# Attention scores from queries and keys split into a high and a low part: three fp32r products in place of one fp32 product

## The chip, the core and the metric

The kernel runs on one NeuronCore of one Trainium2 chip. The number that counts is the time of one execution in device microseconds (us), as the median of several runs. Engines are named as in the profile: PE is the matrix engine, PEld its weight loads, DVE the vector engine, ACT the scalar engine, POOL the GpSimd engine, and SP the engine that issues most of the DMAs. Each engine works through its own queue in order, and engines wait for each other by semaphores.

## What is computed

One layer of a hybrid backbone runs on 128 context tokens and 512 latent tokens (8 rows of 64) with 1024 channels. The modulated input goes through one wide projection. One branch is a gated long convolution. The other is attention with 16 heads of 64 channels: the context attends to itself, and each latent query attends to a window of the latent grid and to 128 cached context keys. The change concerns the scores of this attention:

```python
def context_attention(q, k, v):
    ...
    s = jnp.einsum("bqhd,bkhd->bhqk", q, k).astype(jnp.float32) * (HEAD_DIM ** -0.5)
    p = jax.nn.softmax(s, axis=-1).astype(v.dtype)
    ...

def neighbourhood_attention(q, k, v, ctx_k, ctx_v, rpb):
    ...
    s_win = jnp.einsum("brqhd,brkhd->bhrqk", qg, kg).astype(jnp.float32) * scale
    ...
    s_ctx = jnp.einsum("brqhd,bkhd->bhrqk", qg, ctx_k).astype(jnp.float32) * scale
    p = jax.nn.softmax(jnp.concatenate([s_win, s_ctx], axis=-1), axis=-1).astype(v.dtype)
```

The two branches are then gated, projected and merged (`m_h * p_h + m_a * p_a`), go through one more projection and a layer norm, and the keys and values of the context tokens are outputs too.

## The kernel before

**Projections in three products.** Every projection (`proj`, `accumulate`, line 165) multiplies a weight tile by the 640 tokens. Weights and input are each split into a high part, rounded to the type fp32r, and a low part, the rest (`split`, lines 97 and 98: ACT writes the high part, DVE subtracts it). The product is high by high, high by low and low by high, each an fp32r matmul of 320 columns, over eight blocks of 128 channels: 48 matmuls per projection. The result lies in one of two PSUM tiles `mm` (pool `ps_mm`, two buffers). So the projection after next starts only when ACT, or ACT and DVE, have emptied the tile of this one.

**Scores in one fp32 product.** Heads are worked on in pairs j = 0 to 7; the two heads of a pair lie in partitions 0 to 63 and 64 to 127 of the tiles `q{j}` and `k{j}`. `queries(j)` (line 666) copies the projection from PSUM into `q{j}` in four ACT operations with the factor -0.125; `keys(j)` (lines 674 to 678) copies it into `k{j}` in five, loads the cached keys by two DMAs straight into two places of `k{j}`, and sends the context's keys out from `k{j}` by a DMA. `score` (line 756) is one matmul per head with 64 rows and fp32 operands; the profile shows every fp32 matmul as two records. A pair has four blocks of 128 queries (`KWIN`: 320, 384, 384 and 320 keys) and the context's block of 128 keys. `tiled` issues the scores of two blocks; the softmax (`probs`: DVE, ACT, POOL) follows, and `turned` transposes its result on PE one step later.

**Stages.** The order of PE is written by hand only in the prologue and in the eight steps of attention, where `weave` mixes `attend(j)` with the projections of later pairs (`mains`). Elsewhere, and on the other engines, a list scheduler orders the instructions by the order of the program and by when a simulation finds them ready. Before the attention comes the hand-over: `hand_over()` runs the last tiles of the convolution branch (`quarter_tail(3)`), then `queries(0)`, `keys(0)`, `values(0)`, `gate_a(0)`, `queries(1)`, `keys(1)`, `values(1)`. It is woven with the last quarter of the long convolution (`long_conv(3)`, `long_conv_back(3)`) and with `attention_setup()`. The tail of `long_conv_back(3)` is two transposes `yp` (line 603), eight transposes `y` (line 613), and then DVE alone: lines 606, 615, and the gating at 451 and 455.

**Memory.** SBUF is given out in pools on two stacks, left and right. A tile of a new pool whose bytes belonged to closed pools waits, by the framework's rule, for the last use of those pools as a whole. On the left lie `const`, `wp` (raw, high and low weights), `yhp`, and `hwa`, the convolution's smaller pool, some 24.6 KB per partition by its tile sizes. On the right lie `hp` (the input) and below it `hyc` and `hw`, the convolution's large tiles, closed by `hy.close()` at the start of `attention_setup`. Once `hwa` is closed, its place is taken by `slots_l` (even pairs and j = 0) and `slots_r` (odd pairs), each with one tile q, k and v: 2560 + 3584 + 5120 = 11264 bytes per partition. Closing `hy` makes room for `yap` (attention's output) and `at` (its working tiles).

**After the attention.** `mix_h` puts the eight merge gates `mh0` to `mh7` into the q, k and v tiles of `slots_l` and into a pool `rest` of four tiles. The last loops split the outputs of both branches (`yhH`, `yhL`, `yaH`, `yaL`) and run the projections of the merge.

**Start.** `load_pack(1)` loads small constants in one DMA (428 columns) after the first slice of the input, ahead of `zemb`, which the filter network reads.

Of the kernel before, what the change touches and what calls it, by code (L numbers as in the profile page):

```python
# [9 lines left out]
F32 = mybir.dt.float32  # L10
# [6 lines left out]
LP = 128  # L17
# [27 lines left out]
def tile_hyena_natten_step(ctx: ExitStack, tc: tile.TileContext, a, o):  # L45
# [9 lines left out]
    def two(t):  # L55
        return t.rearrange("p (a b) -> p a b", a=2)
# [36 lines left out]
    def aux(name):  # L93
        return ps_ax.tile([P, 512], F32, tag="aux", name=name)
# [152 lines left out]
    def prologue():  # L247
# [27 lines left out]
        for k in range(NK):  # L275
# [382 lines left out]
    def slot(j, tag, name):  # L658
        pool = out["slots_l"] if j % 2 == 0 else out["slots_r"]
        return pool.tile([P, SLOT[tag]], F32, tag=tag, name=name)  # L660

    def queries(j):
        lo, hi, _ = yield from proj(T_Q + j)
        q = out[f"q{j}"] = slot(j, "q", f"q{j}")
        for dst, src in ((PS_, lo[:, PS_]), (blk(0, 2), lo[:, B01]), (blk(2, 5), hi[:, :HALF]), (blk(7, 1), lo[:, B7])):
            nc.scalar.activation(q[:, dst], src, AF.Copy, scale=-0.125)
        yield

    def keys(j):
        lo, hi, _ = yield from proj(T_K + j)  # L670
        k = out[f"k{j}"] = slot(j, "k", f"k{j}")
        for c in (192, 448):
            load_to(k[:, c : c + P], a["ck"][j])
        nc.scalar.activation(k[:, KP], lo[:, PS_], AF.Copy)
        nc.scalar.activation(k[:, 704:768], lo[:, B7], AF.Copy)
        nc.scalar.activation(k[:, :128], lo[:, B01], AF.Copy)
        nc.scalar.activation(k[:, 128:192], hi[:, :64], AF.Copy)
        nc.scalar.activation(two(k[:, 320:832])[:, :, :128], two(hi[:, 64:HALF]), AF.Copy)
        nc.sync.dma_start(o["new_kT"][j], k[:, KP])
        yield  # L680

    def values(m):
# [41 lines left out]
    def attention_setup():  # L724
        nonlocal at, mask
        hy.close()
        yap = out["yap"] = tail.enter_context(tc.tile_pool(name="yap", bufs=1, side="right"))
        ya.extend(row(yap, "ya", f"ya{j}") for j in range(NK))
        at = ac.enter_context(tc.tile_pool(name="at", bufs=1, side="right"))
        mask = at.tile([P, 640], F32, tag="mask", name="mask")  # L730
        load_to(mask[:], a["mask"])
        for i in range(4):
            tm = at.tile([P, 1024], F32, tag=f"tm{i}", name=f"tm{i}")
            for c in (192, 448, 704):
                nc.gpsimd.memset(tm[:, c : c + P], 0.0)
# [16 lines left out]
        nc.gpsimd.tensor_tensor(tm[:, 832:], mask[:, 448:], tb[:, :192], op=ALU.subtract)  # L752
        return tm

    def score(dst, q, k, h):
        nc.tensor.matmul(dst, q[rows(h)], k[rows(h)], start=True, stop=True, skip_group_check=True)  # L756

    def scores(j, b, s):
        lo, hi = KWIN[b]
        for h in range(2):  # L760
            score(s[h][:, : hi - lo], out[f"q{j}"][:, blk(2 * b, 2)], out[f"k{j}"][:, lo:hi], h)

    LIVE = (slice(64, 384), slice(0, 384), slice(0, 384), slice(0, 320))

# [39 lines left out]
    def block_scores(n, s):  # L804
        j, b = divmod(n, 4)
        if b == 0:
            cv = at.tile([P, P], F32, tag="cacheV", bufs=2, name=f"cv{j}")
            load_to(cv[:], a["cv"][:, j * P : j * P + P])
            head[j] = dict(cv=cv, tm=biases.pop(j))
            for h in range(2):  # L810
                score(s[h][:, 384:512], out[f"q{j}"][:, :LP], out[f"k{j}"][:, KP], h)
        scores(j, b, s)

    def block_probs(n, s):
# [85 lines left out]
        yield  # L900

    def mix_h():
        for n in range(NK):
            if n < 3:
                th = slot(0, "qkv"[n], f"mh{n}")
                if n == 2:
                    pair = th
                th = th[:, :NT]
            elif n == 3:
                th = pair[:, NT:]  # L910
            else:
                if n == 4:
                    out["rest"] = left.enter_context(tc.tile_pool(name="rest", bufs=1))
                th = out["rest"].tile([P, NT], F32, tag="mh", bufs=4, name=f"mh{n}")[:]
            ps = (yield from proj(T_MH + n))[2]
            nc.scalar.activation(two(th), ps[:, :, :HALF], AF.Tanh, scale=0.5)
            out[f"mh{n}"] = th
            yield
# [300 lines left out]
```

## Time and profile before

| what | value |
|---|---|
| median of 3 runs | 931.69 us (931.51 to 932.01) |
| the profiled execution, its own time | 931.77 us |
| span of its trace | 930.0 us |
| busy: PE, DVE, ACT, POOL | 914.6, 470.2, 378.5, 144.9 us |
| score matmuls (line 756) | 160 records, 80 matmuls |

The trace covers the span from the first to the last instruction; the execution's own time is 1.8 us longer. In the lists of groups, `x` is a count, and then come the busy time and the mean of one instruction. A matmul's duration in them is that of one alone, from its start until its result is there. As matmuls overlap, what one costs in a row of many is the row's time divided by the count. The chain of waits does this division: each piece begins where the one before it ended. In the timeline, `x4` merges four instructions that follow each other, and the bracket tells how long the engine was idle before, and for whom.

### The profile page before, as it was taken

Reading aid. Unit: us, or ns where it says so; the run is one execution under the profiler, and the core shown is the slowest. Engines: PE = TensorE matmul, PEld = TensorE weight load, DVE = VectorE, ACT = ScalarE, POOL = GpSimd, SP = SyncE. Lnnn points to the kernel's source line nnn. Section 1 sums busy time; section 2 is a strip of 40 time slices with the busy share of each in tenths; the row PEclk is TensorE's granted clock in tenths of the full one; section 3 lists DMA queues with packets and bytes.
Section 4 is the critical chain, followed back from the end, with each engine's and each line's share of the span. In section 5 each row is a group of like instructions: output and inputs, shape, how many; then the busy total and the mean of one; then the engine's idle time right before and its main releaser. Section 6 shows DMA issues by size and latency. Waiting matters only on the chain.

```text
span 930.0 us, 16507 instructions
## 1 busy us (share of the span) xinstructions
PE 914.6 (98%) x6785; PEld 873.0 (94%) x6785; DVE 470.2 (51%) x868; ACT 378.5 (41%) x769; POOL 144.9 (16%) x188
## 2 busy tenths in 40 slices
PE   9999999999999999999999999999999999999996
PEld 7899999999999999999989999999999999999885
DVE  4676775693796675334342432422171223335676
ACT  4485455555544324245454544444261112223300
POOL 0011010110010000464444443242000000000000
PEclk9999999999999999999999999999999999999999
DMA  9966564665465112342222211311123333223631
GB/s 345 349 159 133 128 148 97 134 135 123 100 144 121 57 49 76 100 116 62 59 89 72 66 65 48 92 50 55 60 69 99 132 115 117 84 69 114 204 113 68
DMA packets 37559, 102.63 MB, mean 110 GB/s; under 512 B 4428, under 2 KB 14028, under 8 KB 37485
## 3 DMA queue, kind: packets, MB, share of 16 engines
q1 hardware_dynamic: 33308, 86.88, 29.2%
q0 software_dynamic: 4032, 14.68, 9.7%
q8 instruction: 53, 0.87, 0.4%
q14 instruction: 22, 0.17, 0.1%
q10 hardware_dynamic: 144, 0.03, 0.0%
HBM read 97.90 MB, written 3.67 MB: 109 GB/s over the span
## 4 chain that ended last, share of the span: by engine, by line
PE 94%; DVE 3%; ACT 1%; DMA 1%; SPq 0%; issue 0%; POOLq 0%; POOL 0%; ACTq 0%
PE mm L165 65%; PE out L1043 6%; PE v L695 5%; PE s L756 3%; PE pt L793 2%; PE s L800 2%; PE ve L704 1%; DMA w<-fw 1%; DMA zemb<-zemb 1%; ACT hH L309 1%; PE yb L150 1%; PE yb L152 1%; PE yb L151 1%; PE gate L242 0%; PE fl L380 0%; PE fl L381 0%
## 5 line engine op out<-in xcount | busy, mean ns | idle before, releaser
L165 PE MATMUL mm<-hH,wh 128*128 128x320 f32 x1120 | 263.0, 313 | 2.3 <-ACT hH L309 1.4
L165 PE MATMUL mm<-hH,wl 128*128 128x320 f32 x1120 | 259.0, 310 | 1.1 <-DVE wl L98 1.1
L165 PE MATMUL mm<-hL,wh 128*128 128x320 f32 x1120 | 259.1, 310 | 0.0
L98 DVE TENSOR_TENSOR wl<-raw,wh 128x1024 fp32r<-128x1024 f32 x66 | 82.3, 1249 | 238.6 <-ACT wh L97 238.3
L165 PEld LDWEIGHTS mm<-hH,wh 128*128 128x128 f32 x1120 | 186.4, 188 | 8.7 <-issue 4.9
L165 PEld LDWEIGHTS mm<-hH,wl 128*128 128x128 f32 x1120 | 187.7, 188 | 2.2 <-DVE wl L98 1.8
L165 PEld LDWEIGHTS mm<-hL,wh 128*128 128x128 f32 x1120 | 188.0, 188 | 1.5 <-DVE hL L310 0.8
L97 ACT ACTIVATE wh<-raw 128x1024 fp32r<-128x1024 f32 x66 | 69.9, 1059 | 207.5 <-PE mm L165 101.3
L142 POOL DMA_DIRECT2D wl<-wall x28 | 24.4, 871 | 265.2 <-ACT wl L141 154.9
L143 ACT ACTIVATE wh<-raw 128x1024 fp32r<-128x1024 f32 x28 | 29.7, 1060 | 43.3 <-PE mm L165 43.2
L777 POOL TENSOR_SCALAR p<-p,sm 128x384 f32<-128x384 f32 x32 | 41.8, 1319 | 28.6 <-DVE sm L776 28.6
L1073 POOL TENSOR_TENSOR r<-r,bc 128x64 f32<-128x64 f32 x1 | 0.3, 322 | 249.8 <-ACT r L1072 249.8
L775 ACT ACTIVATE p<-p,sm 128x384 f32<-128x384 f32 x32 | 19.7, 616 | 40.8 <-DVE sm L772 40.6
L470 DVE SCALAR_TENSOR_TENSOR x<-zs,pack,x 128x641 f32<-128x641 f32 x32 | 28.2, 882 | 14.4 <-ACT x L468 14.4
L777 POOL TENSOR_SCALAR edge<-edge,sm 128x320 f32<-128x320 f32 x32 | 34.7, 1095 | 0.0
L795 ACT ACTIVATE pts<-pt 128x384 f32<-128x384 f32 x64 | 26.4, 500 | 15.7 <-PE pt L793 15.6
L141 ACT ACTIVATE wl<-raw 128x1024 fp32r<-128x1024 f32 x28 | 30.0, 1073 | 0.0
L165 PE MATMUL mm<-yhH,wh 128*128 128x320 f32 x128 | 29.9, 315 | 0.0
L165 PE MATMUL mm<-yhL,wh 128*128 128x320 f32 x128 | 29.1, 309 | 0.0
L165 PE MATMUL mm<-yhH,wl 128*128 128x320 f32 x128 | 29.1, 309 | 0.0
L165 PE MATMUL mm<-yaH,wl 128*128 128x320 f32 x128 | 29.1, 309 | 0.0
L165 PE MATMUL mm<-yaL,wh 128*128 128x320 f32 x128 | 29.1, 309 | 0.0
(326 smaller groups left out, 1643.0 us busy)
## 6 DMA issues: line engine op xcount, KB each, us to landing
raw<-wall SPq DMA_DIRECT2D x96, 512.0 KB, 3.7
wl<-wall POOLq DMA_DIRECT2D x28, 512.0 KB, 5.7
ada<-wada SPq DMA_DIRECT2D x16, 512.0 KB, 7.9
gate<-wada SPq DMA_DIRECT2D x8, 512.0 KB, 3.7
wo<-wall SPq DMA_DIRECT2D x8, 512.0 KB, 3.7
xt<-xT SPq DMA_DIRECT2D x8, 320.0 KB, 8.5
dec<-decay SPq DMA_DIRECT2D x20, 128.0 KB, 3.2
x<-xB SPq DMA_DIRECT2D x5, 512.0 KB, 3.7
```

What stands on the lines that cost most here:

```text
L97: hi = nc.scalar.activation(dst_h, src, AF.Copy)
L98: return hi, (eng or nc.vector).tensor_tensor(dst_l, src, f(dst_h), op=ALU.subtract)
L141: nc.scalar.activation(wl, raw[:], AF.Copy, scale=-1.0)
L142: nc.gpsimd.dma_start(wl, a["wall"][i], accum_op=ALU.add)
L143: nc.scalar.activation(wh, raw[:], AF.Copy)
L165: nc.tensor.matmul(ps[hf][:, :HALF], wt[k], x[:, hf * HALF : (hf + 1) * HALF], start=(i == 0 and k == 0), stop=(i == lead[2] and k == NK - ...
L470: nc.vector.scalar_tensor_tensor(d, zs[:, c : c + NG], convw[:, i, c : c + 1], d, op0=ALU.mult, op1=ALU.add)
L695: nc.tensor.matmul(ps[:, t // 2, t % 2 * 256 : t % 2 * 256 + 256], x[:, k, P * t : P * t + P], wk, start=first and t % 2 == 0, stop=last, ...
L756: nc.tensor.matmul(dst, q[rows(h)], k[rows(h)], start=True, stop=True, skip_group_check=True)
L777: nc.gpsimd.tensor_scalar_mul(pv, pv, sm[:, 2:3])
L795: nc.scalar.activation(ptS[:], pt[:, :384], AF.Copy)
L1043: ins = nc.tensor.matmul(dst, m[k][:, c0 : c0 + P], w[:, c : c + n], start=(first and k == 0), stop=(last and k == NK - 1), skip_group_che ...
```

## The change

The tiles `q{j}` and `k{j}` become fp32r tiles with the high part, and new tiles `ql{j}` and `kl{j}` take the low part. `queries` has three ACT operations and three DVE operations, `keys` five splits. The context's keys are copied once more by ACT to a tile `kp` for the output. The cached keys are loaded by one DMA into a `const` tile that shares its place with `pack1`, copied from there to both places by one ACT operation, and subtracted by two DVE operations. `score` issues six fp32r matmuls for a block, alternating between the heads.

The slots grow to five tiles, 17408 bytes per partition each. `slots_r` is opened after `gate_a(0)` instead of beside `slots_l`. `ya` has one buffer fewer, and the pool `rest` is gone: the gates `mh4` to `mh7` move into `ql`, `kl` of `slots_l` and `q`, `ql` of `slots_r`, and `yaL0` into `kl` of `slots_r`. The constants `convw`, `hyd` and `ident` become a third pack, loaded in the fourth step of the prologue.

```diff
 PACKS = (
     (("cc", 16), ("bss", 16), ("sel", 2)),
-    (("fs1", 2), ("fs2", 2), ("fw1", 64), ("fw2", 128), ("convw", 96), ("hyd", 8), ("ident", 128)),
+    (("fs1", 2), ("fs2", 2), ("fw1", 64), ("fw2", 128)),
+    (("convw", 96), ("hyd", 8), ("ident", 128)),
 )
...
-                out["convw"] = out["convw"].rearrange("p (i c) -> p i c", c=4)
...
+            if k == 3:
+                load_pack(2)
+                out["convw"] = out["convw"].rearrange("p (i c) -> p i c", c=4)
...
-    SLOT = dict(q=NT, k=896, v=5 * 256)
+    SLOT = dict(q=NT, ql=NT, k=896, kl=896, v=5 * 256)
...
+    def heads_of(t):
+        return two(t)[:, :, :P]
 
     def queries(j):
         lo, hi, _ = yield from proj(T_Q + j)
-        q = out[f"q{j}"] = slot(j, "q", f"q{j}")
-        for dst, src in ((PS_, lo[:, PS_]), (blk(0, 2), lo[:, B01]), (blk(2, 5), hi[:, :HALF]), (blk(7, 1), lo[:, B7])):
-            nc.scalar.activation(q[:, dst], src, AF.Copy, scale=-0.125)
+        q, ql = out[f"q{j}"], out[f"ql{j}"] = [slot(j, t, f"{t}{j}", F32R) for t in ("q", "ql")]
+        for cs, shape, src in (
+            (slice(0, 256), two, heads_of(lo[:, :384])), (slice(256, 576), whole, hi[:, :HALF]), (slice(576, NT), whole, lo[:, B7]),
+        ):
+            nc.scalar.activation(shape(q[:, cs]), src, AF.Copy, scale=-0.125)
+            nc.vector.scalar_tensor_tensor(shape(ql[:, cs]), src, -0.125, f(shape(q[:, cs])), op0=ALU.mult, op1=ALU.subtract)
         yield
 
     def keys(j):
+        raw = const.tile([P, 196], F32, tag="pack1", name=f"ck{j}")[:, :P]
+        load_to(raw, a["ck"][j])
         lo, hi, _ = yield from proj(T_K + j)
-        k = out[f"k{j}"] = slot(j, "k", f"k{j}")
-        for c in (192, 448):
-            load_to(k[:, c : c + P], a["ck"][j])
...
+        k, kl = out[f"k{j}"], out[f"kl{j}"] = [slot(j, t, f"{t}{j}", F32R) for t in ("k", "kl")]
+        for cs, shape, src in (
+            (slice(704, 768), whole, lo[:, B7]), (slice(0, 128), whole, lo[:, B01]), (slice(128, 192), whole, hi[:, :64]),
+            (slice(320, 832), heads_of, two(hi[:, 64:HALF])), (KP, whole, lo[:, PS_]),
+        ):
+            split(shape(k[:, cs]), shape(kl[:, cs]), src)
+        kp = const.tile([P, P], F32, tag="kp", name=f"kp{j}")
+        nc.scalar.activation(kp[:], lo[:, PS_], AF.Copy)
+        nc.sync.dma_start(o["new_kT"][j], kp[:])
+        nc.scalar.activation(heads_of(k[:, 192:704]), raw.unsqueeze(1).to_broadcast([P, 2, P]), AF.Copy)
+        for cs in (slice(192, 320), slice(448, 576)):
+            nc.vector.tensor_tensor(kl[:, cs], raw, f(k[:, cs]), op=ALU.subtract)
         yield
...
         out["slots_l"] = left.enter_context(tc.tile_pool(name="slots_l", bufs=1))
+        yield from chain(queries(0), keys(0), values(0), gate_a(0))
         out["slots_r"] = left.enter_context(tc.tile_pool(name="slots_r", bufs=1))
-        yield from chain(queries(0), keys(0), values(0), gate_a(0), queries(1), keys(1), values(1))
+        yield from chain(queries(1), keys(1), values(1))
...
-        ya.extend(row(yap, "ya", f"ya{j}") for j in range(NK))
+        ya.extend(row(yap, "ya", f"ya{j}", bufs=NK) for j in range(NK))
...
-    def score(dst, q, k, h):
-        nc.tensor.matmul(dst, q[rows(h)], k[rows(h)], start=True, stop=True, skip_group_check=True)
+    def score(dst, j, qs, ks):
+        q, ql, k, kl = (out[f"{t}{j}"] for t in ("q", "ql", "k", "kl"))
+        for i, (x, y) in enumerate(((q, k), (ql, k), (q, kl))):
+            for h in range(2):
+                nc.tensor.matmul(dst[h], x[rows(h), qs], y[rows(h), ks], start=i == 0, stop=i == 2, skip_group_check=True)
...
     def mix_h():
+        homes = ((0, "q"), (0, "k"), (0, "v"), (), (0, "ql"), (0, "kl"), (1, "q"), (1, "ql"))
         for n in range(NK):
...
+            th = slot(*homes[n], f"mh{n}") if homes[n] else th
+            th, pair = (pair[:, NT:], None) if n == 3 else (th[:, :NT], th)
...
-        yaL.append(row(out["yap"], "ya", f"yaL{n}", F32R))
-        split(yaH[n][:], yaL[n][:], ya[n][:])
+        yaL.append(row(out["yap"], "ya", f"yaL{n}", F32R, NK)[:] if n else slot(1, "kl", "yaL0", F32R)[:, :NT])
+        split(yaH[n][:], yaL[n], ya[n][:])
```

More of the change, by code (lines that the diff above doesn't have):

```diff
@@ L655, in tile_hyena_natten_step, with slot, whole @@
     PS_ = slice(PC, PC + LP)
-    SLOT = dict(q=NT, k=896, v=5 * 256)
-    def slot(j, tag, name):
+    SLOT = dict(q=NT, ql=NT, k=896, kl=896, v=5 * 256)
+    def slot(j, tag, name, dt=F32):
         pool = out["slots_l"] if j % 2 == 0 else out["slots_r"]
-        return pool.tile([P, SLOT[tag]], F32, tag=tag, name=name)
+        return pool.tile([P, SLOT[tag]], dt, tag=tag, name=name)
+    def whole(t):
+        return t
+    def heads_of(t):
+        return two(t)[:, :, :P]
     def queries(j):
@@ L677, in keys @@
-        nc.scalar.activation(k[:, 128:192], hi[:, :64], AF.Copy)
-        nc.scalar.activation(two(k[:, 320:832])[:, :, :128], two(hi[:, 64:HALF]), AF.Copy)
-        nc.sync.dma_start(o["new_kT"][j], k[:, KP])
+        k, kl = out[f"k{j}"], out[f"kl{j}"] = [slot(j, t, f"{t}{j}", F32R) for t in ("k", "kl")]
[4 more added lines that the diff above has]
+            split(shape(k[:, cs]), shape(kl[:, cs]), src)
@@ L753, in bias_tile @@
         return tm
-    def score(dst, q, k, h):
-        nc.tensor.matmul(dst, q[rows(h)], k[rows(h)], start=True, stop=True, skip_group_check=True)
+    def score(dst, j, qs, ks):
[3 more added lines that the diff above has]
+                nc.tensor.matmul(dst[h], x[rows(h), qs], y[rows(h), ks], start=i == 0, stop=i == 2, skip_group_check=True)
     def scores(j, b, s):
         lo, hi = KWIN[b]
-        for h in range(2):
-            score(s[h][:, : hi - lo], out[f"q{j}"][:, blk(2 * b, 2)], out[f"k{j}"][:, lo:hi], h)
+        score([t[:, : hi - lo] for t in s], j, blk(2 * b, 2), slice(lo, hi))
     LIVE = (slice(64, 384), slice(0, 384), slice(0, 384), slice(0, 320))
@@ L809, in block_scores @@
             head[j] = dict(cv=cv, tm=biases.pop(j))
-            for h in range(2):
-                score(s[h][:, 384:512], out[f"q{j}"][:, :LP], out[f"k{j}"][:, KP], h)
+            score([t[:, 384:512] for t in s], j, slice(0, LP), KP)
         scores(j, b, s)
@@ L902, in mix_h @@
     def mix_h():
+        homes = ((0, "q"), (0, "k"), (0, "v"), (), (0, "ql"), (0, "kl"), (1, "q"), (1, "ql"))
         for n in range(NK):
[L904 to L914, printed above, removed]
+            th = slot(*homes[n], f"mh{n}") if homes[n] else th
+            th, pair = (pair[:, NT:], None) if n == 3 else (th[:, :NT], th)
             ps = (yield from proj(T_MH + n))[2]
```

3 lines of the change are left out of this document (removed).

## The prediction

> **What bounds the kernel now.** I read the page first: span, busy shares, granted clock, and the chain of waits.
>
> ```profile
> span 930.0 us, 16507 instructions
> PE 914.6 (98%) x6785; PEld 873.0 (94%) x6785; DVE 470.2 (51%) x868; ACT 378.5 (41%) x769; POOL 144.9 (16%) x188
> PEclk9999999999999999999999999999999999999999
> PE 94%; DVE 3%; ACT 1%; DMA 1%; SPq 0%; issue 0%; POOLq 0%; POOL 0%; ACTq 0%
> ```
>
> PE is busy for 98% of the span and makes up 94% of the chain. So a microsecond of PE saved is a microsecond of time, and a microsecond in which PE stands still is lost. Busy times by stage come next.
>
> ```profile
> 326.00:352.00 26.00, 25.46 (x203) 25.20 (x201) 20.80 (x25) 8.54 (x20) 0.00 (x0) 1.00 0.15 49
> 394.00:520.00 126.00, 125.83 (x996) 116.66 (x997) 46.08 (x159) 60.47 (x172) 62.88 (x71) 1.00 0.26 78
> ```
>
> The columns are stretch, length, then busy time and count of PE, PEld, DVE, ACT, POOL. In the attention (second row) PE is full, DVE has 80 of 126 us free and ACT 66. In the hand-over (first row) DVE has only 5 of 26 us free. The scores themselves stand in the chain of waits, with the projections beside them:
>
> ```profile
> 338.75 9.24 PE v L695 x77
> 394.00 1.61 PE s L756 x12
> 460.41 5.28 PE mm L165 x36
> 465.70 1.38 PE s L756 x8
> 618.95 1.61 PE s L756 x12
> 637.61 1.38 PE s L756 x8
> ```
>
> Each of the eight pairs has one group of 12 records (context block, 320 and 384 keys; 1.61 us) and one of 8 (384 and 320 keys; 1.38 us): 8 x 2.99 = 23.9 us of PE.
>
> **The scores.** First I check whether the two heads run side by side today. The filter network has an fp32 matmul that uses 64 rows and has no partner:
>
> ```profile
> L203 PE MATMUL ps_f<-hf,pack x4: 429/429/533, 33.3 to 34.2; 64*128 64x320 f32 x4
> L756 PE MATMUL s<-k,q x160: 272/430/587, 393.9 to 638.6; 64*128 64x320 f32 x64, 64*128 64x384 f32 x64, 64*128 64x128 f32 x32
> ```
>
> Its four records start over 0.9 us, 0.30 us apart, for 320 columns. The eight records of a score group follow each other in 1.38 / 8 = 0.17 us, for 352 columns on average. So records of the two heads overlap in pairs. Now the price per column. The 12-group has four 128-column records more than the 8-group and takes 0.23 us more: 0.115 us for a pair of records. An fp32r matmul of 320 columns takes 5.28 / 36 = 0.147 us and one of 256 takes 9.24 / 77 = 0.120, a line of 0.42 ns per column plus 13 ns; 384 columns give 0.173. The fp32 record streams its columns twice: at 0.84 ns per column plus the 8 ns by which 0.115 exceeds 128 x 0.84, a pair of records takes 0.33 us at 384 columns and 0.28 at 320. Two pairs of each make 1.21 us of the 1.38; 0.17 us of entry and exit remain per group.
>
> After the change the heads alternate, and a block takes three paired products. The 8-group takes 3 x (0.173 + 0.147) + 0.17 = 1.13 us, 0.25 less. The 12-group adds three products of 128 columns, at 0.066 by the line or 0.115 by the row of today. I take 0.115, because that row is of the same width and the same weight loads: 1.13 + 0.35 = 1.48, 0.13 less. The sum over eight pairs is 8 x 0.38 = **-3.0 us**. With 0.066 it is -4.2. If fp32r matmuls of the two heads don't overlap, the groups take 6 x 0.320 + 0.17 = 2.09 and 2.49 to 2.78 us, together 1.6 to 1.9 more per pair: +12.7 to +15 us. The overlap is shown for fp32 only; but what shares the array there, two sets of 64 rows, is the same in fp32r, so I take it.
>
> The Trainium skill, "FP8 and Floating Point Precision", section "TensorE Precision Notes", says that a true fp32 product goes through the array in four passes, so three products would take three quarters of the streamed time. By that rule the 1.21 us become 0.91 instead of 0.96, and the sum -3.5 instead of -3.0. The trace gives the fp32r pass 13 ns of its own, so I keep the rows.
>
> **The hand-over.** Here the change moves something past something. By the tile sizes in the code, two sets of slots took 22.5 KB and lay inside the 24.6 KB of the closed pool `hwa`. They now take 34.8 KB, so `slots_r` reaches into the place of `hw`, which lives until the long convolution's last operation. Do pools wait as a whole? Two places show it:
>
> ```profile
> 374.95 0.38 PE L603 MATMUL yp<-pack,yep 128*128 128x128 f32 x2
> 377.51 0.64 PE L695 MATMUL v<-wh,hH 128*128 128x256 f32 x4
> 369.52 0.87 ACT L666 ACTIVATE q<-mm 128x128 f32<-128x128 f32 x4
> 371.77 0.39 ACT L599 ACTIVATE yep<-yb 128x256 f32<-128x256 f32 x1 [1.38 <-PE yb L152]
> 378.43 1.41 DVE L455 TENSOR_TENSOR yh<-yh,u 128x64 f32<-128x64 f32 x4
> 379.77 1.20 DVE L98 TENSOR_TENSOR wl<-raw,wh 128x1024 fp32r<-128x1024 f32 x1
> 380.12 1.81 POOL L735 MEMSET tm<- 128x128 f32 x12 [89.00 <-DMA new_kT<-k]
> ```
> ```profile
> 673.37 0.69 ACT L916 ACTIVATE mh<-mm 128x640 f32<-128x640 f32 x1
> 675.32 0.28 DVE L838 TENSOR_TENSOR ya<-sg,op 128x128 f32<-128x128 f32 x1
> 675.77 1.37 ACT L97 ACTIVATE yhH<-yh 128x640 fp32r<-128x640 f32 x2 [1.71 <-DVE ya L838]
> ```
>
> The first `tm` tile of `at` needs no data, POOL had been idle for 89 us, and yet it is cleared only at 380.12, right after DVE's last use of `u` in `hw` (378.43 + 1.41 = 379.84); the DMA that the bracket names reads `k1` and has no share in that place. And `yhH`, whose input was ready long before, is first written when the attention's last DVE operation is done (675.60). So I expect the first write to `q1` to wait for 379.84. Today it happens at 369.52. Until it is done, the PSUM tile of `queries(1)` stays taken. `keys(1)` has the second one, and `values(1)`, which starts at 377.51 today, must have the first. PE has nothing else in its order there, since the attention's steps come after.
>
> What `q1` costs once it may start: three ACT operations in place of four (0.87 us), each followed on DVE by its low part. Prices for DVE:
>
> ```profile
> L475 DVE SCALAR_TENSOR_TENSOR sg<-sg,mm x8: 797/814/821, 361.6 to 620.1; 128x640 f32<-128x640 f32 x8
> L606 DVE SCALAR_TENSOR_TENSOR u<-u,hyd,yp x8: 340/343/348, 150.2 to 375.6; 128x128 f32<-128x128 f32 x8
> L98 DVE TENSOR_TENSOR wl<-raw,wh x66: 1204/1226/1746, 11.1 to 852.5; 128x1024 fp32r<-128x1024 f32 x66
> ```
>
> That is 0.92 ns per element plus 0.23 us: 0.46, 0.52 and 0.28 us for 256, 320 and 64 columns, less about 0.08 each where one begins under the end of the one before (379.77 against 379.84 above), so 1.1 us, which starts some 0.5 us after the release. PE goes on at 379.84 + 0.2 + 0.5 + 1.1 = 381.6 instead of 377.51: 4.1 us. Upward: the weight split of 1.2 us may stand ahead of them on DVE, and the low parts of `q0` and `k0` (ten operations, 2.6 us at these prices) land in the stretch where DVE is busy 20.8 of 26 us and can push the long convolution's tail. That makes 7.9 at most. Downward: `yep` was ready at 372.16, but its transpose ran at 374.95; were it run at once, 1.3 remain. I take 4.1 and a third of the 2.6: **+5.0 us**.
>
> Something comes back behind it. When PE enters the attention it waits for a split that runs slow:
>
> ```profile
> 393.43 0.56 PE L165 MATMUL mm<-hH,wl 128*128 128x320 f32 x2 [0.78 <-DVE wl L98]
> 391.63 3.28 DVE L98 TENSOR_TENSOR wl<-raw,wh 128x1024 fp32r<-128x1024 f32 x2 [10.66 <-ACT wh L97]
> ```
>
> Two splits take 3.28 us here, against 1.226 each elsewhere, while POOL builds the bias tiles. POOL's start hangs on 379.84 and isn't shifted, PE's is; the splits then run beside an idle POOL: **-0.5 us** (between 0 and -0.8).
>
> **The rest.** In the attention, each pair adds ten DVE operations (2.6 us) and two on ACT; the free 80 and 66 us of 126 cover them. Without that cover six pairs would cost 16 us. But the PSUM tile of a projection is now released by DVE too, in DVE's order. The gate tile `sg` already works so, and there it shows:
>
> ```profile
> 470.81 0.82 DVE sg L475
> 471.77 2.88 PE mm L165 x18
> ```
>
> A projection on PE began at 471.77, only after DVE's `sg` in the chain. For twelve tiles of that kind I add **+0.5 us** (0 to 2.5). Edits that I cost at nothing: the score's later copies have a pair's time of reserve; `keys` has one DMA less on SP's queue and waits for a `const` tile long free; the gates' new homes hold tiles of pairs 6 and 7 whose last scores run 20 us before; `yaL0` and the lost buffer of `ya` only move.
>
> ```profile
> GB/s 345 349 159 133 128 148 97 134 135 123 100 144 121 57 49 76 100 116 62 59 89 72 66 65 48 92 50 55 60 69 99 132 115 117 84 69 114 204 113 68
> pack<-pack SPq DMA_DIRECT2D x1, 214.0 KB, 5.8
> ```
>
> The pack: 232 of 428 columns, 116 KB, move behind three more input slices on SP. At 345 GB/s `zemb` lands 0.3 us earlier, and the same bytes stand ahead of later slices: 0, within 0.3.
>
> **Sum.** 931.77 (the profiled execution; its span is 930.0, and 1.8 us lie around it; the median is 931.69, 0.08 lower) - 3.0 + 5.0 - 0.5 + 0.5 = **933.8 us**. With the bounds: 931.8 - 4.2 + 1.3 - 0.8 = 928.1 to 931.8 - 3.0 + 7.9 + 2.5 = 939.2, where the ends don't come together; 931 to 937 is this case's own range.
>
> **Rivals.**
> *The wait is hidden.* If `slots_r` waits for nothing late, because pool waits follow the bytes (the place that `q1` takes may have been idle long before) or because the scheduler runs `yp` at once and finishes the tail before 376, then PE loses nothing in the hand-over: 931.8 - 3.0 - 0.5 = 928.3 us, faster. It decides once `q1` is emptied before 377.5. The clearing of `tm` at 380.12 speaks against the first way, the idle DVE ahead of the tail for the second.
> *The heads don't overlap in fp32r.* The scores then don't get shorter, the change doesn't do what it says: 933.8 + 3.0 + 12.7 to 15 = about 950 us. For it: no row shows fp32r with 64 rows. Against: line 756 overlaps in fp32.
> *The standing PE loses its clock.* Rows at the end and the start:
>
> ```profile
> 921.60:926.00 4.40, 0.01 (x1) 0.00 (x0) 4.14 (x11) 0.73 (x2) 0.32 (x1) 1.00 0.00 0
> 927.00:930.00 3.00, 0.00 (x0) 0.00 (x0) 0.00 (x0) 0.00 (x0) 0.00 (x0) 0.50 0.37 126
> 1.57 3.64 PE L259 MATMUL adaT<-hid 128*128 128x256 f32 x16 [1.57 <-POOL hid L253]
> ```
>
> PE stopped at 921.6, and the granted clock was still 1.00 until 926 and 0.50 from 927: about 5 us of standing still halve it. At the start sixteen matmuls of 256 columns took 3.64 us, 0.23 each against the 0.120 of later. A stall of 4 to 5 us comes near that. Coming back at half speed for such a stretch costs half of 3.6, 1.8 us: 935.6. The Trainium skill, "TensorE: Matmul & The Clock Gate", section "What's actually happening", says that an idle window of some 3.4 us on a free-running grid halves the clock; the 5 us above agree with it, and by it a stall of 4 us would halve the clock in some runs.
>
> **How the numbers follow.** The wait in the hand-over with paired heads: 0.58. Hidden: 0.24. No overlap: 0.08. The wait with a halved clock: 0.10. What a measurement of this kernel can tell from no change is about 0.2%, 1.9 us: below 929.8 is faster, above 933.6 slower. Faster: nearly all of the hidden case and a little of the main one, 0.25. The main case lies around 933.8, a good half of it above the bound: slower takes that, the halved clock and the lost overlap, 0.48; the same, 0.27. The range from 928.0 to 937.5 holds the hidden case, the main one and the halved clock, and leaves out the lost overlap.
>
> **What would show it.** Right: in the changed trace PE stands still for 4 to 6 us between `keys(1)` and `values(1)`, ACT's copy into `q1` comes right after DVE's last line 455, and score groups take 1.1 and 1.5 us. Wrong: `q1` written near 369 (hidden case), score groups of 2 us and more (no overlap), gaps on PE ahead of projections all over the attention (the release by DVE costs more than 0.5).

## The result, and the profile after

The changed kernel takes 936.53 us (median of 6 runs, 936.18 to 936.98), the kernel before 931.6 us in the same session (930.97 to 932.55). The ratio is 1.0049, with a 95% interval of [1.0039, 1.006]: the change costs 4.9 us. The profiled execution took 936.62 us against 931.77.

The head of the page after the change:

```profile
span 934.8 us, 16765 instructions
PE 915.5 (98%) x6865; PEld 880.6 (94%) x6865; DVE 491.4 (53%) x948; ACT 385.4 (41%) x777; POOL 143.9 (15%) x188
PEclk9999999999999999899999999999999999999999
PE 93%; DVE 3%; ACT 2%; issue 0%; POOL 0%; POOLq 0%; ACTq 0%
```

PE is still the bound. One digit is new: an 8 in the row of the granted clock, in slice 17, which covers about 374 to 397 us. That is the end of the hand-over. The busy times by stage of the kernel after (stretch, length, busy time and count of PE, PEld, DVE, ACT and POOL, then the granted clock) point there too:

```profile
326.00:352.00 26.00, 24.89 (x198) 24.68 (x197) 21.46 (x32) 7.98 (x19) 0.00 (x0) 1.00 0.16 49
352.00:394.00 42.00, 36.92 (x255) 36.42 (x255) 19.39 (x35) 11.95 (x24) 9.41 (x28) 0.92 0.34 96
394.00:520.00 126.00, 125.55 (x1047) 120.57 (x1045) 53.49 (x176) 62.57 (x165) 58.10 (x64) 1.00 0.24 71
```

In the first stretch PE idles 1.11 us, in the second 5.08. The timeline of PE after the change names these places; the bracket is the idle time and what ended it:

```profile
349.21 0.38 PE L721 MATMUL ve<-wh,hH 128*128 128x256 f32 x1 [1.11 <-ACT v L717]
353.70 0.56 PE L166 MATMUL mm<-hH,wh 128*128 128x320 f32 x2 [0.76 <-ACT v L724]
383.51 1.19 PE L712 MATMUL v<-wh,hH 128*128 128x256 f32 x4 [4.31 <-DVE ql L678]
401.34 0.56 PE L166 MATMUL mm<-hH,wl 128*128 128x320 f32 x2 [0.27 <-DVE wl L99]
```

The second row has a twin before the change, of 0.71 us. The first and the third are new, the fourth was 0.78. The chains of waits allow the sum to be closed. First the kernel before (the twin from its timeline, then its chain), then the chain of the one after:

```profile
352.17 0.56 PE L165 MATMUL mm<-hH,wh 128*128 128x320 f32 x2 [0.71 <-ACT v L707]
...
377.67 11.52 PE v L695 x96
...
675.00 0.22 PE op L800 x4
```
```profile
383.51 14.10 PE v L712 x96
...
401.89 0.25 PE s L777
...
679.93 0.22 PE op L820 x4
```

Counted from the span's start, PE is 1.53 us later at the matmul after `ve0` (352.17 before, 353.70 after), and 1.11 of that is the new wait ahead of `ve0`. The wait ahead of `values(1)` adds 4.31. The 96 matmuls of `values(1)` take 14.10 us in place of 11.52, 2.58 more. The wait at the entry of the attention gives 0.51 back. From the first score to the attention's last product on PE it was 675.00 - 394.00 = 281.00 us, and it is 679.93 - 401.89 = 278.04: 2.96 less. The sum is 1.53 + 4.31 + 2.58 - 0.51 - 2.96 = +4.95, and the last products did move by 679.93 - 675.00 = 4.93.

The scores' own groups in the chain after the change:

```profile
442.62 1.16 PE s L777 x11
457.74 1.49 PE s L777 x16
```

A group of two blocks takes 1.16 us (1.38 before), one with the context's block 1.49 (1.61 before). Over eight pairs that is 8 x 0.34 = 2.7 us, nearly all of the attention's 2.96.

The hand-over in the timelines of ACT, POOL and DVE after the change:

```profile
379.42 0.38 ACT L677 ACTIVATE q<-mm 128x256 fp32r<-128x256 f32 x1 [7.89 <-DVE yh L458]
380.01 1.05 ACT L98 ACTIVATE wh<-raw 128x1024 fp32r<-128x1024 f32 x1
382.48 0.28 ACT L98 ACTIVATE k<-mm 128x128 fp32r<-128x128 f32 x1 [0.98 <-DVE kl L99]
382.88 0.22 ACT L677 ACTIVATE q<-mm 128x64 fp32r<-128x64 f32 x1
```
```profile
379.59 1.51 POOL L753 MEMSET tm<- 128x128 f32 x10 [88.42 <-DVE yh L458]
```
```profile
377.86 1.45 DVE L458 TENSOR_TENSOR yh<-yh,u 128x64 f32<-128x64 f32 x4
381.09 1.22 DVE L99 TENSOR_TENSOR wl<-raw,wh 128x1024 fp32r<-128x1024 f32 x1 [0.43 <-ACT wh L98]
382.37 0.48 DVE L678 SCALAR_TENSOR_TENSOR ql<-mm,q 128x320 fp32r<-128x320 f32 x1
383.14 0.23 DVE L678 SCALAR_TENSOR_TENSOR ql<-mm,q 128x64 fp32r<-128x64 f32 x1
```

DVE's last gating ends at 379.31. ACT had stood for 7.89 us and writes the first piece of `q1` 0.11 us later, and POOL's first `tm` follows: both waited for the same event. The last low part of `q1` ends at 383.37, and PE goes on at 383.51. Between the release and that point lie not the bare copies of `q1` but also the cached keys and the copies of `k1`, which waited for the same pool, and a weight split of 1.05 us on ACT and 1.22 us on DVE.

The clock fell in the middle of this wait. The same view, cut there:

```profile
378.00:382.00 4.00, 1.20 (x9) 0.93 (x7) 3.04 (x8) 2.07 (x5) 2.15 (x16) 1.00 0.36 105
382.00:385.40 3.40, 1.89 (x9) 1.92 (x10) 2.25 (x8) 1.64 (x6) 2.53 (x5) 0.50 0.81 236
385.40:388.80 3.40, 3.40 (x18) 3.40 (x18) 0.00 (x0) 0.02 (x1) 2.05 (x4) 0.50 0.38 125
388.80:392.00 3.20, 3.20 (x28) 3.20 (x28) 0.00 (x0) 0.00 (x0) 2.67 (x5) 0.99 0.12 41
```

The clock is 0.50 from 382.0 to 388.8, and PE works in 5.3 us of that time. At half speed it loses half of these, 2.6 us: the 2.58 of `values(1)`. All six runs had the drop: the granted clock, as the mean of a run, is 0.994 or 0.995 in them, and 0.996 to 0.998 in the runs of the kernel before.

### The profile page after: what moved, and what is told of

Read it like the earlier page. It is cut to its first block, busy times and chain, and to the rows that moved or that the text cites. A ratio compares the mean times of both kernels' runs of the same rounds, so it can differ in the third digit from the quotient of the medians.

```text
span 934.8 us, 16765 instructions
## 1 busy us (share of the span) xinstructions
PE 915.5 (98%) x6865; PEld 880.6 (94%) x6865; DVE 491.4 (53%) x948; ACT 385.4 (41%) x777; POOL 143.9 (15%) x188
## 4 chain that ended last, share of the span: by engine, by line
PE 93%; DVE 3%; ACT 2%; issue 0%; POOL 0%; POOLq 0%; ACTq 0%
PE mm L166 64%; PE out L1054 6%; PE v L712 5%; PE s L777 2%; PE pt L813 2%; PE s L820 2%; PE ve L721 1%; PE adaT L243 1%; ACT hH L312 1%; PE adaT L260 1%; PE yb L151 1%; PE yb L153 1%; PE yb L152 1%; PE gate L243 0%; PE fl L383 0%; PE fl L384 0%
## 5 line engine op out<-in xcount | busy, mean ns | idle before, releaser
L166 PE MATMUL mm<-yaH,wh 128*128 128x320 f32 x128 | 29.2, 309 | 0.0
```

The costliest lines, as they stand in the source:

```text
L166: nc.tensor.matmul(ps[hf][:, :HALF], wt[k], x[:, hf * HALF : (hf + 1) * HALF], start=(i == 0 and k == 0), stop=(i == lead[2] and k == NK - ...
```

## The experiments

The theory after the result: the whole loss comes from three things on PE's queue in the hand-over: the wait of `q1` for a pool whose bytes reach into `hw`, the halved clock behind that wait, and the wait ahead of `ve0`. The gain comes from the scores. Rivals: the loss comes from the moved line by itself, from DVE's part in emptying PSUM all over the attention, or the scores gain for another reason than the two halves of the array working side by side. Each kernel was timed against the kernel before on its chip (931.82, 932.05 and 931.63 us in the three sessions).

**q1 in a pool of its own.** Base: the changed kernel. `q` and `ql` of the odd pairs go to a pool opened beside `slots_l`, inside `hwa`'s place; `k`, `kl`, `v` stay in `slots_r`. No byte more is used, and by the tile sizes `q1` and `ql1` lie at the same bytes as in the changed kernel: behind the 17.4 KB of `slots_l`, up to 22.5 KB of `hwa`'s 24.6. Only their pool is another.

```diff
-        pool = out["slots_l"] if j % 2 == 0 else out["slots_r"]
+        pool = out["slots_l"] if j % 2 == 0 else out["slots_q" if tag in ("q", "ql") else "slots_r"]
...
         out["slots_l"] = left.enter_context(tc.tile_pool(name="slots_l", bufs=1))
+        out["slots_q"] = left.enter_context(tc.tile_pool(name="slots_q", bufs=1))
```

> The changed kernel, with q and ql of the odd pairs in a pool of their own, opened beside slots_l inside the place of hwa; k, kl and v of the odd pairs stay in slots_r, opened after gate_a(0). Same bytes, same operations. Theory (q1 waits for the last use of hw because its pool reaches into that place, PE stands still 4.3 us for it, and the halved clock costs 2.6 us more): the stall and the clock's drop go, PE's granted clock stays at 1.00 through 352 to 394, 936.5 - 4.6 - 2.6 = 929.3 us. Rival (the stall comes from the low parts' work on DVE and ACT, not from the wait): the stall stays near 4 us, 936.5 within 1.

Measured: 929.41 us, ratio 0.9975 [0.9966, 0.9984], 7.1 us less than the changed kernel. In its timelines ACT writes `q1` early, while `k1` in `slots_r` still waits for the gating, and PE's wait ahead of `ve0` stays:

```profile
370.82 0.38 ACT L677 ACTIVATE q<-mm 128x256 fp32r<-128x256 f32 x1
378.87 0.42 ACT L694 ACTIVATE k<-ck 128x256 fp32r<-128x256 f32 x1 [5.37 <-DVE yh L458]
```
```profile
348.61 0.38 PE L721 MATMUL ve<-wh,hH 128*128 128x256 f32 x1 [1.11 <-ACT v L717]
```

The wait ahead of `values(1)` is gone, and with it the drop of the clock. So the pool of `q1` carried the loss (4.31 + 2.58 = 6.9 us in the trace), though no byte of `q1` itself lies in `hw`'s place, and the rest of the change is a gain: -3.0 - 0.5 + 1.1 = -2.4, measured -2.4.

**The wait alone, without the change.** Base: the kernel before, with fp32 scores. The four tiles of `rest` go into `slots_r`, which is opened after `gate_a(0)` and now reaches into `hw`. By the tile sizes only those four tiles lie in `hw`'s place, and the first of them is written at 669.77 us; q, k and v of both slots end at 22.5 KB, inside `hwa`'s 24.6.

```diff
         out["slots_l"] = left.enter_context(tc.tile_pool(name="slots_l", bufs=1))
+        yield from chain(queries(0), keys(0), values(0), gate_a(0))
         out["slots_r"] = left.enter_context(tc.tile_pool(name="slots_r", bufs=1))
-        yield from chain(queries(0), keys(0), values(0), gate_a(0), queries(1), keys(1), values(1))
+        yield from chain(queries(1), keys(1), values(1))
...
-                if n == 4:
-                    out["rest"] = left.enter_context(tc.tile_pool(name="rest", bufs=1))
-                th = out["rest"].tile([P, NT], F32, tag="mh", bufs=4, name=f"mh{n}")[:]
+                th = out["slots_r"].tile([P, NT], F32, tag="mh", bufs=4, name=f"mh{n}")[:]
```

> The kernel before, scores in fp32 as before, with slots_r opened after gate_a(0) and the four tiles of the pool rest made part of slots_r, so that slots_r reaches into the place of hw; nothing else. Theory (the wait alone makes the stall): q1 is written only after DVE's last gating at 379.8, PE stands still 3.4 us ahead of values(1), 0.5 comes back at the first weight splits of the attention: 931.6 + 2.9 = 934.5 us; with a halved clock 937. Rival (the stall needs the low parts): 931.6 within 0.7.

Measured: 936.28 us, ratio 1.0054 [1.0041, 1.0066]. ACT's copy, PE's wait, and the stretch behind it by stage:

```profile
380.21 0.89 ACT L666 ACTIVATE q<-mm 128x128 f32<-128x128 f32 x4 [1.40 <-DVE yh L455]
```
```profile
381.16 1.09 PE L695 MATMUL v<-wh,hH 128*128 128x256 f32 x4 [3.20 <-ACT q L666]
```
```profile
381.30:384.70 3.40, 3.40 (x17) 3.40 (x18) 0.00 (x0) 0.66 (x4) 2.11 (x13) 0.51 0.77 230
```

With four quick copies the wait is 3.20 us, and the clock was halved for 3.4 us all the same. A wait of 3.2, a loss of 1.7 and some 0.5 that comes back at the attention's entry make +4.4; measured +4.5, near the second of the two times expected, the one with a halved clock. The loss needs nothing of the new scores. And `q1` waits for `hw` although only other tiles of its pool reach there: the pool waits as a whole.

**The moved line alone.** The same edit of the order, with the old sizes, so that `slots_r` stays in `hwa`'s place.

```diff
         out["slots_l"] = left.enter_context(tc.tile_pool(name="slots_l", bufs=1))
+        yield from chain(queries(0), keys(0), values(0), gate_a(0))
         out["slots_r"] = left.enter_context(tc.tile_pool(name="slots_r", bufs=1))
-        yield from chain(queries(0), keys(0), values(0), gate_a(0), queries(1), keys(1), values(1))
+        yield from chain(queries(1), keys(1), values(1))
```

> The kernel before, with slots_r opened after gate_a(0) as in the change, but with its old size, so that it lies in the place of hwa alone. My theory: the moved line costs nothing by itself, the wait comes from the bytes that reach into hw: within 0.3 us of the kernel before (931.6), q1 written near 369 as before. Rival: opening a pool later makes its first tile wait for everything ahead of it, wherever it lies: then near the 936.3 us of e2_before_wait.

Measured: 932.1 us, ratio 0.9998 [0.9989, 1.0007]. ACT writes `q1` at 370.25:

```profile
370.25 0.86 ACT L666 ACTIVATE q<-mm 128x128 f32<-128x128 f32 x4
```

Opening the pool later costs nothing. What costs is that the pool's bytes reach into `hw`.

**PE kept busy through the wait.** Base: the changed kernel, with 24 matmuls of 256 columns between `keys(1)` and `values(1)` whose result nobody reads.

```diff
-        yield from chain(queries(1), keys(1), values(1))
+        yield from chain(queries(1), keys(1))
+        warm = aux("warm")
+        for _ in range(24):
+            nc.tensor.matmul(warm[:, :256], hH[:, 0, :P], hH[:, 0, :256], start=True, stop=True, skip_group_check=True)
+        yield from values(1)
```

> The changed kernel, with 24 matmuls of 256 columns, whose result nobody reads, on PE between the projection of keys(1) and values(1), where it stands still. They take 2.9 us of the 4.3. Theory (the clock is halved because PE stands still, and that costs 2.6 us beside the stall): no drop of the granted clock, the stall's end where it was, 933.9 us. Rival (the drop costs nothing, for example because the time at half clock is waiting anyway): 936.5 within 0.5.

Measured: 934.4 us, ratio 1.0028 [1.0019, 1.0038]. PE's wait in its timeline:

```profile
383.16 0.71 PE L712 MATMUL v<-wh,hH 128*128 128x256 f32 x4 [1.46 <-DVE ql L678]
```

`values(1)` starts 0.35 us earlier than in the changed kernel, as `ve0` already did (348.86 against 349.21), but the clock stays at 1.00 through 352 to 394. The difference of the times, 936.5 - 934.4 = 2.1 us, is then the price of the clock; in the chains the 96 matmuls of `values(1)` take 11.75 us in place of 14.10, 2.35 less.

**All copies first, then all low parts.** Base: the changed kernel; in `queries` and `keys` ACT's copies come first and DVE's low parts behind them (shown for `queries`).

```diff
+        low = []
         for cs, shape, src in (
...
             nc.scalar.activation(shape(q[:, cs]), src, AF.Copy, scale=-0.125)
-            nc.vector.scalar_tensor_tensor(shape(ql[:, cs]), src, -0.125, f(shape(q[:, cs])), op0=ALU.mult, op1=ALU.subtract)
+            low.append((shape(ql[:, cs]), src, f(shape(q[:, cs]))))
+        for dst, src, hi_ in low:
+            nc.vector.scalar_tensor_tensor(dst, src, -0.125, hi_, op0=ALU.mult, op1=ALU.subtract)
...
```

> The changed kernel, with the copies of queries and keys in another order: first all of ACT's copies out of the PSUM tile, then all of DVE's low parts, instead of ACT and DVE by turns. Same operations. Theory (by turns, each ACT copy waits for the low part before it, so k0's copies last 13 us and hold up ve0 by 1.1 us, and q1's last 4 us instead of 1.6): no gap at 349, q1's PSUM tile free at 381.1 instead of 383.4, the clock keeps 1.00 if PE then stands still under 3.4 us: 931.5 us; 934 if the clock drops all the same. Rival (the turns cost nothing, the wait for hw is all): gap at 349 stays, 936.5 within 0.7.

Measured: 930.46 us, ratio 0.9985 [0.9976, 0.9994], 6.1 us less than the changed kernel by the order of a few small operations. Why shows in how ACT copies `k0` in the changed kernel and here:

```profile
342.66 0.22 ACT L98 ACTIVATE k<-mm 128x64 fp32r<-128x64 f32 x1 [2.99 <-DVE kl L99]
345.53 0.39 ACT L98 ACTIVATE k<-mm 128x256 fp32r<-128x256 f32 x1 [2.65 <-DVE kl L99]
```
```profile
337.02 0.93 ACT L694 ACTIVATE k<-mm 128x64 fp32r<-128x64 f32 x5
```

In the changed kernel each copy of ACT waits until DVE has read the piece before it from the same PSUM tile, and DVE does a long operation of the convolution in between. The Trainium skill, "PSUM — Partial Sum Buffer", section "PSUM bank collisions raise a hardware error", says that accesses of two engines to one bank and quadrant must not meet, reads included, and that the compiler's scheduler puts a dependency between them; the waits of 2.99 and 2.65 us agree with it. Here the five copies run in 0.93 us. `ve0` then starts without a wait, and the wait ahead of `values(1)` shrinks:

```profile
379.51 0.73 PE L719 MATMUL v<-wh,hH 128*128 128x256 f32 x4 [1.31 <-DVE ql L681]
```

The sum is 1.1 (`ve0`) + 3.0 (4.31 to 1.31) + 2.1 (the clock, by the run before; it stays at 1.00 here) = 6.2. Of the 3.0 us, 2.1 are `q1`'s: PE goes on 2.08 us after DVE's last gating in place of 4.20, with the low parts of `q1` now ahead of the weight split on DVE. The other 0.9 come from the gating itself, which ends 1.88 us earlier (377.43), while PE runs dry only 1.00 us earlier (378.20).

**Both repairs.** 

> Both repairs together: q and ql of the odd pairs in a pool of their own (as in e1_q1_own_pool, 929.4 us) and, in queries and keys, first all copies of ACT, then all low parts of DVE (as in e4_grouped). If the 1.1 us that PE still stands ahead of ve0 in e1_q1_own_pool comes from ACT and DVE taking turns at k0's PSUM tile, the gap goes and the time is 929.4 - 1.1 = 928.3 us. Rival: the gap ahead of ve0 is DVE's total work in that stretch, which the order inside one projection does not change: then 929.4.

Measured: 928.67 us, ratio 0.9957 [0.9943, 0.9971]. Once more, for a profile:

> The kernel of e5_both once more, whose profiled execution was disturbed: 928.3 to 928.9 us, and in the profile PE without the gap of 1.1 us ahead of ve0, if ACT and DVE taking turns at k0's PSUM tile make it.

Measured: 928.35 us, ratio 0.9961 [0.9947, 0.9974], 3.3 us faster than the kernel before and 8 faster than the changed one. From 330 to 396 us the timeline has two pauses of PE of 0.3 us or more: 0.31 us at the attention's entry (392.72), and the one that the kernel before had as well:

```profile
351.95 0.56 PE L166 MATMUL mm<-hH,wh 128*128 128x320 f32 x2 [0.71 <-ACT v L731]
```

**One fp32 product again.** Base: q1 in its own pool.

```diff
-        for i, (x, y) in enumerate(((q, k), (ql, k), (q, kl))):
-            for h in range(2):
-                nc.tensor.matmul(dst[h], x[rows(h), qs], y[rows(h), ks], start=i == 0, stop=i == 2, skip_group_check=True)
+        for h in range(2):
+            nc.tensor.matmul(dst[h], f(q[rows(h), qs]), f(k[rows(h), ks]), start=True, stop=True, skip_group_check=True)
```

> On the base of e1_q1_own_pool (929.4 us): one fp32 product per head of the high parts in place of three fp32r products; the two products with low parts are left out, everything that makes the low parts stays. This isolates the term of the scores: if three products save what the trace says (groups of 1.61 and 1.38 us against 1.49 and 1.16), the time is 929.4 + 8 x 0.34 = 932.1 us. Rival: the groups' shorter time is given back elsewhere in the attention (a softmax that then ends last): then within 1 us of 929.4.

Measured: 933.77 us, ratio 1.0014 [1.0005, 1.0023], some 4 us more than its base, where 2.7 were expected; its groups are back at the old size:

```profile
402.36 1.38 PE s L777 x8
421.31 1.61 PE s L777 x12
```

In the traces 0.88 us of the difference lies already ahead of the attention (`ve0` at 349.49 against 348.61). From the first score to the attention's last product it is 280.81 us against 278.03, 2.78 more, near the expected 2.7. So the term of the scores is confirmed in sign and, in the stretch where it acts, in size.

**Second head on the first head's rows.** Base: q1 in its own pool.

```diff
-                nc.tensor.matmul(dst[h], x[rows(h), qs], y[rows(h), ks], start=i == 0, stop=i == 2, skip_group_check=True)
+                nc.tensor.matmul(dst[h], x[rows(0), qs], y[rows(0), ks], start=i == 0, stop=i == 2, skip_group_check=True)
```

> On the base of e1_q1_own_pool (929.4 us): the products of both heads read rows 0 to 63, so that the second head's scores are computed from the first head's queries and keys and the second head's are left out; as many matmuls of the same sizes. If two sets of 64 rows run side by side because they lie in different halves of the array, this takes the overlap away: an 8-group takes 6 x 0.320 + 0.17 = 2.09 us in place of 1.16, a 12-group 2.5 to 2.8 in place of 1.49, in all 15 to 18 us more: 945 to 947 us. Rival: what overlaps in the trace is only the entry and the exit of neighbouring matmuls, whatever their rows: then 929.4.

Measured: 948.41 us, ratio 1.0175 [1.0161, 1.0189]. The groups in its chain:

```profile
402.46 2.13 PE s L778 x12
422.15 2.82 PE s L778 x18
```

The groups take 0.97 and 1.33 us more, 18.4 for eight pairs; measured are 19.0. Two products on the same 64 rows run one after the other, on different rows beside each other, in fp32r too.

**The order of the heads.** Base: q1 in its own pool. Two versions: first the three products of one head and then those of the other, block by block; and all products of the first head in both blocks ahead of the second head's.

```diff
-        for i, (x, y) in enumerate(((q, k), (ql, k), (q, kl))):
-            for h in range(2):
+        for h in range(2):
+            for i, (x, y) in enumerate(((q, k), (ql, k), (q, kl))):
```

> On the base of e1_q1_own_pool (929.4 us): the three products of one head follow each other, then those of the other head. If matmuls of 64 rows run side by side only with a neighbour in the other half of the array, only the products at the borders between heads pair up: an 8-group then takes 1.6 to 2.1 us in place of 1.16, a 12-group 2.1 to 2.75 in place of 1.49, together 1.0 to 2.1 us more for each of eight pairs: 937.5 to 946 us. Rival: the order in the queue doesn't matter to the overlap: 929.4.

Measured: 929.62 us, ratio 0.997 [0.9958, 0.9982]: no loss. My expectation was wrong, its rival right. A group in this kernel's timeline:

```profile
401.79 0.45 PE L778 MATMUL s<-k,q 64*128 64x384 f32 x2
402.07 0.34 PE L778 MATMUL s<-k,ql 64*128 64x384 f32 x2
402.24 0.35 PE L778 MATMUL s<-kl,q 64*128 64x384 f32 x2
```

The queue holds three products of one head and then three of the other, but the trace has them side by side. The second version moves the partners 6 and 9 places apart:

```diff
...
-        for n in ns:
-            block_scores(n, ss[n])
+        for h in range(2):
+            for n in ns:
+                block_scores(n, ss[n], (h,))
```

> On the base of e1_q1_own_pool (929.4 us): all products of the first head in both blocks of a step, then all of the second head: the partner of a matmul now stands 6 or 9 places behind it in the queue, and 3 in e6_head_by_head, which lost nothing (929.6). If the two halves of the array take matmuls as two independent streams from a queue that looks further ahead than 9, 929.4 to 930. If the look-ahead ends between 3 and 9, part of the group runs alone: up to 0.16 us for each product without a partner, 938 to 946 us where none of them has one but at the border.

Measured: 939.01 us, ratio 1.0076 [1.0064, 1.0089]. Groups in the chain, and the start of one in the timeline:

```profile
402.13 1.61 PE s L778 x11
421.30 2.23 PE s L778 x17
```
```profile
402.06 0.44 PE L778 MATMUL s<-k,q 64*128 64x384 f32 x1
402.34 0.33 PE L778 MATMUL s<-k,ql 64*128 64x384 f32 x1
402.51 0.34 PE L778 MATMUL s<-kl,q 64*128 64x384 f32 x1
402.52 0.49 PE L778 MATMUL s<-k,q 64*128 64x384 f32 x2
```

The groups take 0.45 and 0.74 us more than in the base, 9.5 for eight pairs; measured are 9.6. The first head has one product k,q of 384 columns in this group; the second such product, which starts at 402.52, is the second head's first one. (Its line merges it with the fourth in the queue, the first head's k,q of 320 columns, which starts behind it.) It stands seventh in the queue and starts with the third (402.51), before the fourth. So here PE looked four places ahead for the other half of the array; three places, as in the version before, are hidden, six are not. That each engine works through its own queue in order, as was said at the start, does not hold for these matmuls.

## Why the prediction came out as it did

The forecast was 933.8 us, the result 936.5: the right side, 2.7 us short. It lies within the stated range, but by the room left there and not by the sum: the sum has no term for the halved clock.

- **Scores, -3.0.** Right. Groups of 1.13 and 1.48 us were worked out, 1.16 and 1.49 measured, and for three products of 128 columns the row of the same width was the right choice of the two. The premise that heads overlap in fp32r was argued then; the run with both heads on the same rows shows it. The other estimate for the same term, -3.5, counts the shorter streaming for one of a pair's two groups; counted for both it is -3.8, farther from the 2.7 that the groups saved.
- **The wait in the hand-over, +5.0.** The mechanism is right and shown three ways: `q1` waits for the last use of the closed pool, giving `q1` another pool at the same bytes takes the loss away, and the wait put into the kernel before makes it lose as much. The rival that pool waits follow the bytes of a tile is out with that: `q1` lies in `hwa`'s place in all of these kernels. Two sizes were off and partly cancelled. PE ran dry at 379.20 (383.51 - 4.31) in place of the 377.51 of before, so it had less to wait. But `q1` took 3.95 us from its first copy (379.42) to its last low part (383.37), where 1.6 was reckoned: the split that I held only as an upper bound did stand ahead, and ACT and DVE took turns with the copies of `k1`, which the sum had not counted. In all 4.31 us, against 4.1 plus a third of 2.6.
- **The low parts of `k0`, inside that third.** These were to push the convolution's tail past the 379.84 of before. They did not: its last gating ended at 379.31 (with all copies first it ends at 377.43, so the order did hold it up, but not past that mark). They held up ACT instead, and so `ve0`: 1.11 us. The run with all copies first shows the cause. At the prices given the ten operations come to 2.9 us, not 2.6, which would have moved the forecast by 0.1.
- **The halved clock.** This is the step that failed: it was a rival with a chance of 0.10 and a price of 1.8 us, and it came, at 2.58 us in the trace and 2.1 by the run that keeps PE busy. I had taken the 5 us at the kernel's end as the nearest row for how long PE may stand. That row ends in a drop but does not say that a shorter pause is safe; 3.20 us were enough. Added to the sum, this term would have given 935.9 to 936.4; that this comes so close is in part luck, as the other terms' errors cancel.
- **The entry of the attention, -0.5.** Right in size: the wait went from 0.78 to 0.27 us, and the two splits took 1.23 us each beside an idle POOL. But PE's shift was not needed for it. With `q1` in its own pool PE enters the attention at nearly its old time (the split's matmul starts at 393.83, before 393.43), and the wait is 0.26 us as well. There POOL ends its bias tiles at 389.95, ahead of both splits; in the kernel before it waits 1.65 us for the last bias table and ends at 393.83, in the middle of them. Why that table lands earlier, no run isolates. This is also why the time of the hidden wait, 928.3, which has the -0.5 without a shift, is what the kernel with both repairs reaches (928.67 and 928.35).
- **Release of PSUM by DVE in the attention, +0.5.** Nothing there: the attention shortened by 2.96 us, and the groups alone explain 2.7. The cost of that kind lay in the hand-over, where DVE is full.
- **Packs, cached keys, homes, at nothing.** No row of theirs stands in the sum above. 0.42 us of the 1.53 up to `ve0` have no cause that a run isolates; the starts of the experiments differ by as much (`ve0` at 348.39 to 349.49 in kernels that are alike up to there).

## What to carry to other kernels

A pool whose tiles grow can reach into the place of a pool that is closed later, and then the first write to any of its tiles waits for that pool's last use: look at where the pool's bytes end, and give the tile that is written first a pool that ends in the place that is free first. A pause of PE can have two prices, its own length and a stretch of half speed behind it: here 1.7 us behind a pause of 3.20, and 2.1 to 2.6 behind one of 4.31. Where two engines empty one PSUM tile, let the idle engine read all its pieces first, so that the busy one isn't asked once per piece.

## What the runs showed that I had not expected

- PE pairs 64-row matmuls of the two halves of the array even where they are not neighbours in its queue: at a distance of 3 places nothing is lost (929.62 against 929.41 us), at 6 and 9 places 9.6 us are, and the second head's first product starts with the one four places ahead of it.
- Pauses of 3.20 and 4.31 us halved the clock, for 3.4 and 6.8 us; pauses of 1.31 and 1.46 us did not. The Trainium skill, "TensorE: Matmul & The Clock Gate", section "What's actually happening", speaks of windows of some 3.4 us on a free-running grid, and of a halved clock after at least one idle window; the lengths of the drops agree with the windows. That a whole window has to be idle does not show here: one pause was 3.20 us long, and behind the start of the other (379.20) the clock fell after 2.8 us.
- In one profiled execution (both heads on the same rows) the clock was also halved where PE had no pause of more than 0.3 us, for 3.4 us once:

```profile
594.50:595.20 0.70, 0.70 (x6) 0.70 (x5) 0.49 (x2) 0.22 (x1) 0.00 (x0) 1.00 0.96 369
595.20:598.60 3.40, 3.40 (x28) 2.82 (x26) 1.89 (x10) 1.89 (x9) 1.62 (x3) 0.50 0.50 172
```

No run tells why.
